# A two-layer hybrid backbone on one core: the same instructions, ordered by another scheduler model

## The chip, the cores and the metric

The kernel runs on one core of a Trainium2 chip. The metric is the device time of one execution in microseconds (us). Three timed runs of the kernel before took 2687.60, 2689.13 and 2694.43 us; the median, 2689.13, is the time that the prediction speaks of.

## What is computed

The input is 256 latent tokens and 256 context tokens of 1024 channels. Two layers of this block run one after the other, and a final RMSNorm gives the latent tokens:

```
h   = modulate(rmsnorm(x), shift, scale)              # adaLN: shift, scale, gate from c
u   = h @ w_in                                        # one combined input projection
mix = [rwkv7 (both directions), gla (both directions, chunks of 64),
       windowed attention (sink and context keys), s5 (both directions)]
y   = sum_i sigmoid(h @ w_gate_i) * (mix_i(u) @ w_branch_i)
x   = x + gate * (y @ w_out)
h2  = modulate(rmsnorm(x), ...)
x   = x + gate * moe(h2)    # top-1 group of 4, top-2 of its 8 experts, hidden 512
```

Everything is float32 to within its last bits: many products are done as a pair of a rounded part and its remainder (`hh`, `hl`; `yh`, `yl`; `bh`, `bl`).

## The kernel before, in words

`layer` (L1734) writes one layer down in this order: the first norm, the adaLN products (`adaln`, L1232: a 512 KB block of w_ada is loaded and meets eight small matmuls into `ada`, whose sum goes to `mods`), S5 (`s5`, L1033), GLA (`gla`, L634, with the chunk sums `pc<-cst,ke` at L731), the RWKV projections (`rwkv_in`), attention (`attn`), the eight RWKV units (`rwkv_units`, L360), and the gated merges of the four mixers (`merge`, L1336). Merges 1, 3 and 2 (GLA, S5, attention) need nothing of the units; merge 0 needs their output `yT[0]`. Then come the output projection and the second norm (`tail`, L1569) and the mixture of experts (`moe`, L1608; a pair of experts in `pair`, L1496). Layer 0 works on 512 tokens after the mixers, layer 1 on the 256 latent ones.

A unit (`rwkv_sub`, L463) is one half of the heads, one direction, one stream; there are 2 x 2 x 2 per layer, and here they are called U0 to U7 in layer 0 and V0 to V7 in layer 1. A unit is a long chain. TensorE makes scores (`psc`), VectorE and ScalarE copy them (`sm`), a DMA sends their diagonal blocks to device memory (`ad`, L510), another spreads them over the partitions (`lt`, L513), VectorE inverts the blocks in 62 operations of which each needs the one before:

```
for t in range(31):
    n = 31 - t
    self.tt(tm[:, :, 0:n], lt[...], ti[...], OP.mult)
    self.tt(ti[:, :, t + 1:32], ti[:, :, t + 1:32], tm[:, :, 0:n], OP.add)
```

DMAs bring the result back transposed (`td`, L524, and `tT`, L529), and TensorE runs eleven small groups (`psp`, `psy`, `psz`, `psv`, `psta`, `psav`, `pst`, `psq`, `psh`, `pss`, `psyo`) with copies by other engines between them. After every four units `rwkv_finish` (L410, matmuls `pc`) norms and gates a half. While a unit waits for VectorE or a DMA, TensorE has the merges' gate products to do: `pa`, sixteen or more matmuls for each 512 KB of gate weights (`g`, then the pair `gs`).

Nobody writes the order of the instructions by hand. The program is traced in the order of the code, and the tile layer's scheduler then picks, for each engine, the next instruction from those whose inputs and buffers its model of the machine has ready; where several are ready, the one that stands first in the code goes first. So the merges, which stand behind the units in the code, fill what the model thinks idle. Each engine, and each DMA queue (nearly all loads go through SP's), executes its list strictly in that order. The change touches the call that opens this scheduler, at L1869.

Of the kernel before, what the change touches and what calls it, by code (L numbers as in the profile page):

```python
# [46 lines left out]
def _consts():  # L47
# [3 lines left out]
    s = p % 64  # L51
# [15 lines left out]
    # sums of the four partial rows: row r of layer l  # L67
# [4 lines left out]
    # unit columns 4 (p % 8) .. + 3 of a 32-token block  # L72
# [14 lines left out]
def pack(i):  # L87
# [18 lines left out]
    def cols(a):  # L106
        """128 columns a tile: [l, n, 128, 8, 128]"""
        return a.reshape(L, 128, 8, -1, 128).transpose(0, 3, 1, 2, 4)

    def rows(a):  # L110
        """256 columns of half of the rows a tile: [l, n, 2, 128, 4, 256]"""
        return a.reshape(L, 128, 2, 4, -1, 256).transpose(0, 4, 2, 1, 3, 5)
# [6 lines left out]
    # query heads in the order 0, 2, 1, 3  # L119
# [53 lines left out]
class Net:  # L173
# [18 lines left out]
    def psum(self, name, **bufs):  # L192
        """A pool for the eight banks, cut into rotating sets."""
        self.pbufs = bufs
        cm = self.tc.tile_pool(name=name, bufs=1, space=PSUM, reuse_waits="tile")
        self.ps = cm.__enter__()
        return cm
# [4 lines left out]
    def const(self, c, n, pool):  # L202
        """Constants that one part alone needs."""
        t = pool.tile([128, n], F32, name="const")
        self.nc.scalar.dma_start(t, self.io["cst"][:, c:c + n])
        return t
# [10 lines left out]
    def wtile(self, src, pool):  # L217
        """A weight tile [128, k, n] of at most 8 KB on each partition."""
# [5 lines left out]
    def gload(self, src, pool=None):  # L224
        """A granule [128, k, n] of weights, of at most 4 KB on each partition."""
# [8 lines left out]
    def gsplit(self, src):  # L234
        """The granule as an exact pair for the tensor engine."""
# [10 lines left out]
    def mm3(self, out, a, b, start, stop):  # L246
        """Product of two exact pairs: all but the product of the two remainders, below float32's last bit."""
# [4 lines left out]
    def proj(self, out, src, h, a):  # L252
        """Channel-major projection: out = 128 columns of the weights, tokens a .. 511."""
# [7 lines left out]
    def rowpair(self, src):  # L261
        """256 columns of weights: the pair of each k."""
# [27 lines left out]
    # ------------------------------------------------------------------ RWKV  # L290
    def rwkv_in(self, l, h, lo, pool, tp, between):
        """Projection, centered shift and low-rank projections; what the units need."""
# [18 lines left out]
        # per-partition (scale, offset) that make the rate into the two stacked key factors  # L311
# [27 lines left out]
        # low-rank projections of xa  # L339
# [15 lines left out]
    def rwkv_first(self, l, st, pool):  # L355
        """What the first units need."""
# [23 lines left out]
    def unit_tiles(self, st, p0, pool, depth):  # L380
        """Tiles of the units whose constant parts are written once."""
# [16 lines left out]
    def rwkv_half(self, l, hf, st, pool):  # L398
        """Minus the normalized key direction of two heads."""
# [10 lines left out]
    def rwkv_finish(self, l, hf, st, y, pool):  # L410
        """Group norm over each head, gain, bonus, gate."""
# [23 lines left out]
    def rwkv_pre(self, hf, d, st, pool):  # L435
        """Decay and in-context rate of both streams, in scan order: the decays' products within a chunk,
        their inverses, and the two stacked key factors."""
# [19 lines left out]
        # the sums are used up: their place takes the first factor  # L457
# [5 lines left out]
    def rwkv_sub(self, hf, d, s, u, S0, st, na, y, pool):  # L463
        """One stream of one direction: four chunks of 64 tokens. S0: the state before it."""
# [28 lines left out]
        # scores (transposed) with token-major copies of the keys beside them  # L493
# [11 lines left out]
        # inverse of the 32-token diagonal blocks: four columns of one block a partition  # L505
# [24 lines left out]
        # off-diagonal quarter of the 64-token inverse  # L530
# [28 lines left out]
        # token-major values beside the solved block  # L559
# [13 lines left out]
        # banks of their own: their row tiles differ  # L573
# [31 lines left out]
        # states entering the chunks  # L605
# [27 lines left out]
    # ------------------------------------------------------------------ GLA  # L633
    def gla(self, l, h, yT, lo, pool):  # L634
# [8 lines left out]
        # low-rank decay input first: it heads the longest chain  # L643
# [29 lines left out]
        # log decays of both directions  # L673
# [29 lines left out]
    def gla_dir(self, d, la, q, kx, v, mg, oT, lo, pool):  # L703
# [23 lines left out]
        # per-chunk state increments  # L727
# [28 lines left out]
        # block-diagonal entering states of two heads; scores block-diagonal over the chunks of a token tile  # L756
# [41 lines left out]
    # ------------------------------------------------------------- attention  # L798
    def attn(self, l, h, yT, lo, pool):
# [8 lines left out]
        # queries and keys of a token tile, in places that the probabilities take later  # L808
# [34 lines left out]
        for a in range(2):  # L843
            ps = self.pa()
            for t in range(t0, 4):
                # heads a and a + 2: one for each key/value head
                nc.tensor.transpose(ps[:, 128 * t:128 * t + 128], qk[t][:, 128 * a:128 * a + 128], ident)
            self.act(qT[:, a, 128 * t0:512], ps[:, 128 * t0:512], AF.Copy, scale=0.125)
        # heads a + 2 g: a pair of row groups for the scores, of column groups for the sums
# [40 lines left out]
    # -------------------------------------------------------------------- S5  # L890
    def cmul(self, o, a, b, t, eng=None):
        """o = a * b for pairs (re, im) of views; t: two scratch views."""
# [8 lines left out]
    def sincos(self, out, ang, shift, pool, name):  # L901
        """out = sin(ang + shift), the angle reduced to [-pi, pi] in three exact steps."""
# [36 lines left out]
    def s5_params(self, l, ld, t2, pool):  # L939
        """Powers of the discrete transition, the input matrix and the chunk-scan tables."""  # L940
# [26 lines left out]
        # unit rotation over a chunk of eight tokens  # L967
# [5 lines left out]
        # (a - 1) / lam  # L973
# [25 lines left out]
    def s5_head(self, l, ld, pool):  # L999
        """What depends on the parameters alone."""  # L1000
# [12 lines left out]
    def s5_table(self, pr, d, pool):  # L1013
        """Powers 0 .. 63 of the rotation over a chunk."""
# [18 lines left out]
    def s5(self, l, h, w, yT, lo, pool, pr):  # L1033
# [6 lines left out]
        # chunks of eight tokens: ug[(t, channel), group, chunk]  # L1040
# [48 lines left out]
    def s5_quarter(self, d, gb, lo, pr, tb, ug, ys, kd, t2, dd, pool):  # L1089
        """One direction of eight groups: four pairs of groups."""  # L1090
# [20 lines left out]
        # input matrix times powers, in the order of a chunk's tokens  # L1111
# [9 lines left out]
        # impulse response within a chunk  # L1121
# [22 lines left out]
        # states at chunk ends, rotated into a frame where the scan is real  # L1144
# [13 lines left out]
        # z = f * conj(rotation)  # L1158
# [15 lines left out]
        # states entering each chunk, in token order  # L1174
# [21 lines left out]
        # within the chunk and from the entering state: banks of their own, their tiles differ  # L1196
# [22 lines left out]
    # --------------------------------------------------------- conditioning  # L1219
    def cond(self):  # L1220
        """silu of both conditioning vectors, channel-major, padded to a 32-column tile."""
# [10 lines left out]
    def adaln(self, l, js, pool=None, bank="A"):  # L1232
        """Tiles js of the layer's modulations. mods: rows (layer, modulation, stream), four partial sums of each."""
# [11 lines left out]
    def modcols(self, l, ks, mc, ps):  # L1245
        """Channel-major scale and shift of the first norm, mc: [128, scale/shift, stream, 8], for blocks ks."""
# [9 lines left out]
    def rstd(self, xs, pool, name, bufs=1):  # L1256
        """1 / rms of each token of the [128, 1024] tiles xs, by Newton's iteration."""
# [17 lines left out]
    def norm1(self, xs, xn, pool, then):  # L1275
        """Normalized tokens xn; then(k, their transposes in a PSUM bank)."""
# [13 lines left out]
    def modulate(self, k, mc, h, src, tmp):  # L1290
        """Modulated tokens as an exact pair."""
# [6 lines left out]
    def rows(self, l, pool):  # L1298
        """Rows of the modulations and of the second norm's scale, as exact pairs for the tensor engine."""
# [20 lines left out]
    def bcast(self, rw, r, half):  # L1320
        """PSUM bank holding half a row on every partition."""
# [6 lines left out]
    # ---------------------------------------------------------------- merge  # L1328
    def split(self, pool, tags, src, bufs=1, eng=None):
        """src as an exact pair for the tensor engine."""  # L1330
# [5 lines left out]
    def merge(self, l, i, h, yT, acc, lo, first, pool, between, pairs=None):  # L1336
        """acc (channel-major) += (1 + tanh(gate / 2)) * branch: twice the gated branch."""
# [27 lines left out]
    def project(self, t, w, acc, x, bs, lo, pool):  # L1365
        """x += modulation * (merged @ w_out) for a token tile."""
# [11 lines left out]
    # ------------------------------------------------------------------ MoE  # L1378
# [494 lines left out]
```

## Time and profile before

| | |
|---|---|
| median of three timed runs | 2689.13 us |
| span of the profiled execution | 2682.7 us |
| outside the span, against the median | 6.4 us |
| TensorE (PE) busy | 2425.7 us, 90% |
| VectorE (DVE) busy | 1257.7 us, 47% |
| ScalarE, GpSimd busy | 651.6 and 708.5 us |
| moved by DMA | 553.6 MB, 206 GB/s on the mean |

The profiled execution has no time of its own beside its span; all sums are made against the span. From the timeline, in us from the span's start: layer 0 has its front (norm, adaLN, S5, GLA, RWKV projections, attention) to 364, the units with the merges to 646, the last merge to 785, the tail to 882 and its experts to 1480; layer 1 has its front to 1785, the units to 2079, the last merge to 2116, the tail to 2180 and the experts to the end. TensorE is the engine that is nearly always busy, so the time is its work plus its idle stretches; each of these has a reason that a view of the waits names.

### The profile page before, as it was taken

To read this page: it belongs to the slowest core of one execution; us is meant where nothing else is said; L and a number is where in the kernel's file an instruction comes from. 1 tells how busy PE (TensorE), PEld (TensorE's weight loads), DVE (VectorE), ACT (ScalarE), POOL (GpSimd) and SP (SyncE) were. 2 spreads that over 40 slices of the span, in tenths; PEclk is the share of its full clock that TensorE was granted. 3 is DMA by queue.
4 is the path that set the end of the run, shared out by engine and by line. 5 is a ranking of instruction groups with operands and counts; after the bars stand their busy time and mean duration, and the time that the engine had idled before them with its cause. 6 is when DMAs were issued, how large, how long until landed. Compare 5 with 4: busy or idle time off the path is not lost. (4 is left out here: it accounts for less than half of the span.)

```text
span 2682.7 us, 41783 instructions
## 1 busy us (share of the span) xinstructions
PE 2425.7 (90%) x16663; PEld 1460.5 (54%) x16663; DVE 1257.7 (47%) x3477; ACT 651.6 (24%) x1147; POOL 708.5 (26%) x609
## 2 busy tenths in 40 slices
PE   6889989989898999999998788987988989999997
PEld 5766756567654545444443676765766644333332
DVE  6575488883224433222223766478665342212212
ACT  2232543222212111111111332441222311111111
POOL 2224411133421233133313333431133411111121
PEclk8987989999999899999999887887688989999999
DMA  6332212124543698888884342322222779999994
GB/s 218 105 112 87 67 49 66 51 63 161 200 149 115 278 390 345 312 333 325 325 347 196 114 143 84 115 64 72 62 81 64 255 310 419 411 395 402 399 398 172
DMA packets 143947, 553.59 MB, mean 206 GB/s; under 512 B 33236, under 2 KB 64340, under 8 KB 93316
## 3 DMA queue, kind: packets, MB, share of 16 engines
q1 hardware_dynamic: 138480, 544.88, 53.9%
q10 hardware_dynamic: 5268, 5.97, 0.7%
q8 instruction: 135, 2.21, 0.3%
q14 instruction: 64, 0.52, 0.1%
HBM read 546.66 MB, written 4.13 MB: 205 GB/s over the span
## 5 line engine op out<-in xcount | busy, mean ns | idle before, releaser
L267 PE MATMUL pa<-hh,gs 128*128 128x512 f32 (+2 forms) x1440 | 446.6, 383 | 19.5 <-DVE sg L283 8.6
L273 POOL TENSOR_TENSOR gs<-g,gs 128x1024 fp32r<-128x1024 f32 (+1 forms) x106 | 255.4, 2413 | 570.5 <-PE pa L267 271.2
L273 POOL TENSOR_TENSOR ta<-ta,mb 128x512 f32<-128x512 f32 x93 | 127.8, 1381 | 834.4 <-ACT ta L270 834.4
L267 PEld LDWEIGHTS pa<-hh,gs 128*128 128x128 f32 (+1 forms) x1440 | 270.6, 202 | 83.2 <-issue 15.8
L267 PE MATMUL pd<-w,hT 128*64 128x512 f32 x1024 | 276.6, 599 | 13.1 <-ACT hT L270 12.4
L267 PE MATMUL pa<-hl,gs 128*128 128x512 f32 (+2 forms) x720 | 270.9, 387 | 0.0
L267 PE MATMUL pgate<-w,xT 128*64 128x512 f32 x1024 | 251.3, 596 | 0.0
L267 PE MATMUL pup<-w,xT 128*64 128x512 f32 x1024 | 249.2, 594 | 0.0
L267 PEld LDWEIGHTS <-h2p 128*128 128x128 bf16 x2304 | 134.3, 99 | 77.9 <-issue 72.5
L270 ACT ACTIVATE gs<-g 128x1024 fp32r<-128x1024 f32 (+1 forms) x106 | 110.4, 1045 | 258.0 <-PE pa L267 175.9
L267 PE MATMUL pg<-oh,h2p 128*128 128x128 bf16 x2304 | 162.6, 222 | 5.8 <-DVE nv L1652 4.2
L267 PEld LDWEIGHTS pa<-hl,gs 128*128 128x128 f32 (+1 forms) x720 | 148.1, 206 | 28.3 <-issue 9.6
L267 PEld LDWEIGHTS pd<-w,hT 128*64 128x64 f32 x1024 | 81.6, 136 | 146.7 <-issue 124.3
L267 PEld LDWEIGHTS pup<-w,xT 128*64 128x64 f32 x1024 | 78.4, 137 | 143.1 <-issue 138.9
L267 PEld LDWEIGHTS pgate<-w,xT 128*64 128x64 f32 x1024 | 74.8, 137 | 139.6 <-issue 129.4
L267 PE MATMUL py<-yp,oT 128*128 128x512 f32 x384 | 132.2, 438 | 11.2 <-ACT ta L270 5.1
L283 DVE SCALAR_TENSOR_TENSOR hd<-hd,pgate 128x512 f32<-128x512 f32 x32 | 22.0, 687 | 246.4 <-ACT hd L270 246.3
L273 DVE TENSOR_TENSOR tm<-lt,ti 128x76 f32<-128x76 f32 (+27 forms) x496 | 132.3, 286 | 5.9 <-DMA lt<-ad 0.8
L273 DVE TENSOR_TENSOR ti<-ti,tm 128x76 f32<-128x76 f32 (+28 forms) x496 | 128.1, 277 | 5.0
L273 DVE TENSOR_TENSOR hd<-hd,pup 128x512 f32<-128x512 f32 x32 | 22.0, 687 | 218.0 <-PE pup L267 218.0
L273 POOL TENSOR_TENSOR x<-x,ta 128x512 f32<-128x512 f32 x93 | 121.5, 1313 | 4.9
L283 DVE SCALAR_TENSOR_TENSOR yp<-pd,ws,yp 128x512 fp32r<-128x512 f32 x64 | 47.7, 746 | 152.6 <-ACT yp L270 152.6
(495 smaller groups left out, 3736.2 us busy)
## 6 DMA issues: line engine op xcount, KB each, us to landing
w<-in_w_g SPq DMA_DIRECT2D x128, 1024.0 KB, 8.2
w<-in_w_d SPq DMA_DIRECT2D x128, 1024.0 KB, 10.2
w<-in_w_u SPq DMA_DIRECT2D x128, 1024.0 KB, 8.5
g<-in_w_ada SPq DMA_DIRECT2D x96, 512.0 KB, 3.8
g<-in_w_in_gate SPq DMA_DIRECT2D x64, 512.0 KB, 3.6
g<-in_w_in_rwkv SPq DMA_DIRECT2D x16, 512.0 KB, 3.6
lt<-ad SPq DMA_DIRECT2D x16, 512.0 KB, 4.4
wb<-in_w_branch SPq DMA_DIRECT2D x64, 128.0 KB, 3.0
```

The source lines that it names most:

```text
L267: self.nc.tensor.matmul(out, lhsT, rhs, start=start, stop=stop, skip_group_check=True)
L270: self.nc.scalar.activation(out, in_, f, **kw)
L273: (eng or self.nc.vector).tensor_tensor(out, a, b, op)
L283: self.nc.vector.scalar_tensor_tensor(out, a, s, b, op0=op0, op1=op1)
```

## The change

The scheduler that orders the instructions is told to use its event-by-event model of all devices (engines, queues and semaphores) in place of its plain model. That is one argument. The rest of the diff takes out comments and docstrings and leaves blank lines in their place, so that line numbers stay.

```diff
-    with tile.TileContext(nc) as tc:
+    with tile.TileContext(nc, schedule_with_timeline_sim=True) as tc:
         build(tc, nc, io, out)
```

Both programs hold the same 20,889 instructions, with the same names, on the same engines; what differs is each engine's order (and, with it, the number of waits that stand apart as instructions: 494 and 461 on PE, 364 and 351 on DVE, 731 and 759 on SP). Three places on PE show what moves.

The first is the end of the units of layer 1, on PE. `tT_15196` belongs to V6 and `tT_15197` to V7; `ar_15192` and `ar_15193` likewise; `pa` is merge work. Before:

```order
L267 MATMUL pa<-hh,gs 128x256
L267 MATMUL psq<-sm,x_15194 64x64
L267 MATMUL psp<-cst,tT_15197 32x32 x7
L267 MATMUL pa<-hl,gs 128x256
L267 MATMUL pa<-hh,gs 128x256 x2
L267 MATMUL psq<-sm,x_15194 64x64 x7
L267 MATMUL psh<-x_15194,sm 64x64 x8
L267 MATMUL psy<-tp,sm 32x32 x8
L267 MATMUL pa<-hh,gs 128x256 x4
L267 MATMUL pss<-h_16884,qg 64x64 x2
```

And now:

```order
L267 MATMUL psc<-ar_15192,bk 128x192 x2
L267 MATMUL psc<-ar_15193,bk 128x192 x8
L267 MATMUL psp<-cst,tT_15196 32x32 x8
L267 MATMUL psy<-tp,sm 32x32 x8
L267 MATMUL psz<-tT_15196,ysb 32x32 x8
L267 MATMUL psv<-cst,vv 64x64 x8
L267 MATMUL psta<-cst,ar_15192 64x64 x8
L267 MATMUL psav<-x_15194,sm 64x64 x8
L267 MATMUL psp<-cst,tT_15197 32x32
L267 MATMUL pst<-bk,tT_15196 64x128 x8
L267 MATMUL psp<-cst,tT_15197 32x32 x7
```

The scores of V7 are now directly ahead of V6's `psp`, and no merge matmul stands between there and V7's finish; before, 161 `pa` matmuls stood between V7's scores and its `psp` and 245 up to its finish. The merge work that stood here has been moved ahead of V7's scores.

The second is the end of the units of layer 0, on PE (`tT_3388` belongs to U6, `x_3386` to U6, `x_3387` and `tT_3389` to U7). Before:

```order
L267 MATMUL pa<-hh,gs 128x512 x5
L267 MATMUL pst<-bk,tT_3389 64x128 x8
L267 MATMUL pa<-hh,gs 128x512 x2
L267 MATMUL pa<-yh,bh 128x512
L267 MATMUL pa<-yl,bh 128x512
L267 MATMUL psq<-sm,x_3387 64x128
L267 MATMUL pa<-yh,bl 128x512
L267 MATMUL pa<-yh,bh 128x512
L267 MATMUL psq<-sm,x_3387 64x128 x7
```

And now:

```order
L267 MATMUL pa<-hh,gs 128x512 x8
L267 MATMUL psp<-cst,tT_3388 32x32 x8
L267 MATMUL psy<-tp,sm 32x32 x8
L267 MATMUL psz<-tT_3388,ysb 32x32 x8
L267 MATMUL psv<-cst,vv 64x64 x8
L267 MATMUL psta<-cst,ar_3383 64x64 x8
L267 MATMUL psav<-x_3386,sm 64x64 x8
L267 MATMUL pst<-bk,tT_3388 64x128 x8
L267 MATMUL psq<-sm,x_3386 64x128 x8
L267 MATMUL psh<-x_3386,sm 64x64 x8
```

From U7's last scores there are 35 merge matmuls up to the first row of this piece, and none from it to U7's finish; then 14 are left of merges 1 to 3. Before, 174 merge matmuls stood between U7's scores and its finish, and 238 of merges 1 to 3 behind it.

The third is the end of merge 0 in layer 0, on PE: adaLN products of layer 1's modulation that are spread through merge 0. `pa<-w,acc` is the output projection of the tail; eight `ada` matmuls use one 512 KB block. Before:

```order
L267 MATMUL pb<-yl,bh 128x512
L267 MATMUL pb<-yh,bl 128x512
L267 MATMUL bs<-mods,cst 128x512 x2
L267 MATMUL ada<-g,cT 32x128 x8
L267 MATMUL pa<-w,acc 128x512
L267 MATMUL bs<-mods,cst 128x512 x2
L267 MATMUL mod<-mods,cst 12x512
L267 MATMUL pa<-w,acc 128x512
```

And now:

```order
L267 MATMUL pb<-yl,bh 128x512
L267 MATMUL pb<-yh,bl 128x512
L267 MATMUL pa<-w,acc 128x512 x4
L267 MATMUL ada<-g,cT 32x128 x16
L267 MATMUL pa<-w,acc 128x512 x12
L267 MATMUL ada<-g,cT 32x128 x32
L267 MATMUL bs<-mods,cst 128x512 x2
L267 MATMUL ada<-g,cT 32x128 x32
L267 MATMUL bs<-mods,cst 128x512 x2
L267 MATMUL mod<-mods,cst 12x512
```

Ten blocks of w_ada are now used behind merge 0's last matmul, and one was before.

## Rows read from the trace of the kernel before

**Rows 1.** The page, busy time of an engine, share of the span, instructions.
```profile
PE 2425.7 (90%) x16663; PEld 1460.5 (54%) x16663; DVE 1257.7 (47%) x3477; ACT 651.6 (24%) x1147; POOL 708.5 (26%) x609
```

**Rows 2.** Busy time by stretch: units with merges, of layer 0 and layer 1.
```profile
core 0: us, PE busy (x) PEld busy (x) DVE busy (x) ACT busy (x) POOL busy (x), PEclk, DMA share, GB/s
364.00:785.00 421.00, 389.84 (x2984) 272.93 (x2981) 247.96 (x792) 112.29 (x196) 123.67 (x67) 0.95 0.36 117
...
1785.00:2116.00 331.00, 285.57 (x2441) 227.94 (x2440) 216.76 (x738) 88.95 (x166) 103.14 (x69) 0.80 0.32 97
```

**Rows 3.** Timeline around U7, layer 0: start, length, engine, line, operation.
```profile
562.82 0.92 PE L267 MATMUL psc<-ar,bk 64*128 64x192 f32 x4
...
568.09 0.56 SPq L513 DMA_DIRECT2D lt<-ad  x1
...
601.62 0.17 DVE L273 TENSOR_TENSOR ti<-ti,tm 128x4 f32<-128x4 f32 x1
...
609.49 0.43 PE L267 MATMUL psp<-cst,tT 32*32 32x32 f32 x14
...
644.06 0.39 PE L267 MATMUL pa<-hl,gs 128*128 128x512 f32 x1
644.29 0.39 PE L267 MATMUL pa<-hh,gs 128*128 128x512 f32 x1
...
644.84 1.12 PE L267 MATMUL pc<-sg,g 64*128 64x512 f32 x2
```

**Rows 4.** The page: groups of the 62 operations, and the DMA of lt.
```profile
L273 DVE TENSOR_TENSOR tm<-lt,ti 128x76 f32<-128x76 f32 (+27 forms) x496 | 132.3, 286 | 5.9 <-DMA lt<-ad 0.8
L273 DVE TENSOR_TENSOR ti<-ti,tm 128x76 f32<-128x76 f32 (+28 forms) x496 | 128.1, 277 | 5.0
...
lt<-ad SPq DMA_DIRECT2D x16, 512.0 KB, 4.4
```

**Rows 5.** Busy time by stretch: U7's and V7's chain, and V7's last part.
```profile
564.00:646.00 82.00, 73.30 (x631) 51.31 (x631) 55.31 (x172) 21.75 (x35) 24.14 (x13) 0.96 0.20 60
...
2000.00:2078.50 78.50, 64.44 (x620) 53.65 (x621) 49.99 (x165) 20.16 (x33) 26.36 (x19) 0.85 0.30 87
2049.00:2078.50 29.50, 29.50 (x341) 22.87 (x338) 10.81 (x28) 10.29 (x16) 7.75 (x6) 1.00 0.16 46
```

**Rows 6.** PE groups by line: units' second parts (15 groups), a finish (3 groups).
```profile
L267 PE MATMUL psq<-sm,x 128*64 128x128 f32 (+1 forms) x256 | 23.6, 279 | 2.0 <-DVE x L589 2.0
...
L267 PE MATMUL pc<-s,cst 128*128 128x512 f32 (+1 forms) x16 | 7.6, 559 | 4.8 <-DVE s L283 4.8
...
L267 PE MATMUL pc<-yT,cst 128*128 128x512 f32 (+1 forms) x8 | 3.7, 548 | 0.0
...
L267 PE MATMUL psyo<-qg,h 64*64 64x64 f32 x16 | 1.5, 267 | 0.0
```

**Rows 7.** Timeline: PE's weight loads at a switch between a unit and a merge.
```profile
562.82 0.62 PEld L267 LDWEIGHTS psc<-ar,bk 64*128 64x128 f32 x4 [0.17 <-ACT sm L270]
...
563.66 0.19 PEld L267 LDWEIGHTS pa<-hh,gs 128*128 128x128 f32 x1 [0.22 <-issue]
```

**Rows 8.** Timeline at the end of merge 0, layer 0: adaLN products and their loads.
```profile
744.57 0.64 PE L267 MATMUL ada<-g,cT 128*32 128x128 f32 x16
746.50 0.64 PE L267 MATMUL ada<-g,cT 128*32 128x128 f32 x16
...
751.80 28.48 SPq L231 DMA_DIRECT2D g<-in_w_ada  x10
```

**Rows 9.** Waits of PE: layer 1's front, then layer 0's experts (us, times, longest).
```profile
PE pc L731 <- POOL ke L273: 8.9, 1, 8.9
...
PE ph L1538 <- DVE hd L273: 7.8, 10, 0.8
...
PE pd L267 <- ACT hT L270: 4.9, 10, 0.7
```

**Rows 10.** Busy time by stretch, layer 1's units; the clock is third from the end.
```profile
1785.00:1990.00 205.00, 176.96 (x1501) 134.30 (x1499) 150.65 (x548) 52.19 (x101) 47.53 (x32) 0.74 0.25 70
...
1840.00:1860.00 20.00, 17.62 (x232) 14.07 (x230) 16.08 (x57) 4.93 (x9) 5.45 (x3) 1.00 0.35 100
1860.00:1900.00 40.00, 36.09 (x286) 27.51 (x288) 24.41 (x103) 5.60 (x14) 5.33 (x4) 0.55 0.13 36
```

## The prediction, made before the changed kernel ran

> **What bounds the kernel now.** First the page's busy times: TensorE is at 2425.7 us [rows 1] of a span of 2682.7, so 257 us of idle TensorE are all that an order can win, unless it alters how long the matmuls take. No instruction is added or dropped, so every term below is idle time that comes or goes, and the clock. Second, busy time by stretch: the units with their merges take 421.0 us in layer 0 with TensorE busy 389.8 (31.2 idle), and 331.0 us in layer 1 with 285.6 (45.4 idle) [rows 2]. These are the stretches in which the scheduler has most freedom. Third, the timeline of one unit. U7's last scores end at 563.7, its `lt` load is issued at 568.1, its last inversion step ends at 601.8, `psp` is at 609.5 and its finish ends at 646.0 [rows 3]. That is 82 us of chain, beside which TensorE was busy for 73.3 us. V7's chain takes 78.5 us, with 64.4 us of TensorE work beside it [rows 5]. So a unit's chain is long and almost free of charge, as long as merge work lies beside it. The question to put to the new order is how much of that work still lies there.
>
> **The length of the chain when nothing lies beside it.** From last scores to the first inversion step: issue of `lt` 4.4 us after the scores end [rows 3], landing 4.4 [rows 4], 8.8 together. The 62 steps: 31 x (286 + 277) ns = 17.4 us [rows 4]. From the last step to `psp`'s end: 601.8 to 609.9, 8 us [rows 3]. From there to the finish: 29.5 in layer 1 [rows 5]. Sum 63.7 us, the lower end. The upper end is what was measured with work beside it and another unit's steps taking turns on VectorE: 82 and 78.5 us.
>
> **What now lies beside it.** In layer 0 the order leaves 35 merge matmuls behind U7's scores, which follow each other at 0.23 us (644.06 and 644.29) [rows 3]: 8.1 us. Then U6's and U7's second parts: 15 groups of rows, from 23.6 to 1.5 us for 16 units, sum 180.5, so 11.3 us a unit [rows 6], and a finish, three groups of 7.6, 4.2 and 3.7 us for four finishes, 3.9 us [rows 6]. Together 8.1 + 22.6 + 3.9 = 34.6 us. The chain of 64 to 82 us leaves TensorE idle for 29 to 47. I take 40: U6's scores end over 20 us of matmuls ahead of U7's, so its steps are half done when U7's begin. In layer 1 there is no merge matmul at all: 22.6 + 3.9 = 26.5 us, and idle for 37 to 52. I take 50, near the upper end, since the scores of V6 end only one scores group (3 us) ahead of V7's, so that both units' 35 us of steps share VectorE just as in the measured 78.5 us. What waits behind is everything: PE's list is in order, and merge 0 needs the finish anyway.
>
> **What the moved merge work gives back.** It now lies ahead, among the earlier units, where it covers waits. Of the 31.2 idle us of layer 0's stretch 8.7 lie beside U7's chain (82.0 less 73.3), so 22.5 elsewhere; of layer 1's 45.4, 14.1 beside V7's (78.5 less 64.4), so 31.3 elsewhere [rows 2, 5]. I let 9 and 12 of these remain; the ends are none and all. Then layer 0's stretch goes from 31 to 49 (+18) and layer 1's from 45 to 62 (+17).
>
> **Fewer changes of work.** The new order has TensorE go from merge to unit matmuls or back 116 times in place of 198 in layer 0, and 114 in place of 188 in layer 1. A switch left the weight load idle for 0.17 and 0.22 us [rows 7], of which a part is a true wait; I take half, 0.11: -9 and -8 us. The ends are 0 and -34 for both.
>
> **The adaLN blocks behind merge 0.** Ten blocks of w_ada are used behind merge 0's last matmul in place of one, with only 16 projection matmuls among them. In the trace ten such loads took SP 28.5 us to issue, each waiting for one of two buffers, and the closest blocks ran 1.9 us apart (744.57 and 746.50) [rows 8]. Ten blocks need 19 to 28 us; beside them lie ten times 0.64 us of `ada` and 16 x 0.23 of projection, 10 us. So 9 to 18 us of idle, or none, if loads run ahead or if the second norm has TensorE wait there anyway. I take 12. Before, the same loads were hidden by merge 0's matmuls; that cover is what goes.
>
> **Layer 1's front.** The one long stall there is 8.9 us, `pc` for GLA's `ke` [rows 9], which VectorE reached late because S5's steps stood ahead. The new order moves GLA's steps ahead of more of S5's and puts the first `pc` seven rows earlier, with S5 and adaLN matmuls in place of a bare run of `pa`. -9 us, the ends 0 and -9 (the wait can only go once). Layer 0's front changes as much but had short waits; I take nothing.
>
> **The experts.** The gather of the next pair now stands between `pup` and `ph` or `ph` and `pd` for three more pairs in each layer. The waits it can cover are 7.8 and 4.9 us over ten pairs in layer 0 [rows 9]: three pairs, -4 us. Layer 1's experts are paced by their weight loads; nothing.
>
> **The sum.** +18 +17 -9 -8 +12 -9 -4 = +17 us on a profiled execution of 2682.7, so 2699.7; with the 6.4 us between span and median, 2706 us.
>
> **The clock.** In layer 1's units the granted clock was 0.74 of full on the mean, and it alternated between stretches at the upper of its two levels (1840 to 1860: 1.00, TensorE busy 17.6 of 20) and stretches near the lower one (1860 to 1900: 0.55, busy 36.1 of 40, when it was hardly idle) [rows 10]. So in this trace a dense stretch was not always a fast one, and I put the clock at no change. The bounds: at 0.95, as in layer 0's same stretch [rows 2], the 177 us of matmuls would be 177 x (1 - 0.74/0.95) = 39 us shorter at most; at half clock for the whole of layer 1's merge 0 behind its gap, which takes 36 us now, up to 36 longer. The Trainium skill ("Perfetto Trace Analysis", Matmul Optimizations) says that the engine scales with utilization and that matmuls should run back to back in batches; by that rule the longer batches of the new order would raise the clock, and the first rival below is what comes of it. The skill's "TensorE: Matmul & The Clock Gate" (Part 1, HAM oscillation) speaks the other way: work that follows a wait starts cold, which would make the two long gaps dearer than their own length. The row of 1860 to 1900 agrees with neither by itself.
>
> **The rivals.**
> (a) Faster. The denser filler ahead of V7 lifts layer 1's clock to layer 0's 0.95. Its place is 1785 to 1990, its price -39, and it decides as soon as it gives over 25 us. Sum +17 - 39 = -22: 2667 us. For it: the waits of that stretch are ones that filler covers. Against: the 0.55 at 90% busy.
> (b) No change. U7's and V7's gaps come out at the lower ends (29 and 37, not 40 and 50), and the adaLN blocks hide in the norm's wait: 17 - 11 - 13 - 12 = -19, against which the other waits of the units stay at half (+6) and the switches give nothing back (+17): +4, 2693 us.
> (c) Much slower. Upper ends for the gaps (47 and 52), no stall covered elsewhere (22.5 and 31.3), 18 us for the adaLN blocks: (69.5 - 31.2) + (83.3 - 45.4) + 18 - 17 - 13 = +64, 2753 us. Against: merge matmuls really are put ahead of the earlier units' waits.
> (d) The order is hardly different where it counts, so the change does nothing: excluded by the rows of the order, where hardly a row of PE stands as it did.
>
> **How the numbers follow.** A measurement of this kernel can tell about 0.3% (8 us) from no change: 2681 to 2697. Forecast (2698 to 2732) 0.40; (a) and what lies between it and no change 0.29; (b) and other sums within the 8 us 0.20; (c) 0.11. Faster 0.29, same 0.20, slower 0.51. The range leaves a tenth at either end: half of (a) lies above 2662, and (c) reaches past 2745.
>
> **What would show it.** Right: in the changed trace a gap of 25 us or more on TensorE in each layer with nothing but `ti` and `tm` on VectorE, and `psp` of U6 and V6 released by `tT`; `ada` waiting for `g<-in_w_ada` for about 10 us ahead of layer 0's tail; `psc` waiting less in sum than before; the 8.9 us for `ke` gone. Wrong: TensorE's idle time in 364 to 785 and 1785 to 2116 no larger than 31 and 45 us, or TensorE's busy time changed by over 15 us, which would be the clock.

## The result

The changed kernel takes 2704.1 us (median of 20 runs), the kernel before 2687.5 (median of 20 beside it). The ratio is 1.0067, 95% interval 1.0049 to 1.0084: slower by 0.7%, where 2706 was forecast. How it comes about is another matter, and most of this part is about that. The profiled execution has a span of 2708.3, 25.6 more than the one of before, where the medians differ by 17; the stretches below are compared between these two executions. One kernel's runs differ too (the 20 of the kernel before lie between 2669 and 2698 us), so a few us in a stretch can be chance. The page:

```profile
PE 2419.9 (89%) x16663; PEld 1463.3 (54%) x16663; DVE 1273.8 (47%) x3477; ACT 649.3 (24%) x1147; POOL 692.3 (26%) x609
```

Over the whole run TensorE is busy for 5.8 us less than before [rows 1], so in sum the loss is idle time; by stretch it is not. The ends are those of the same instructions in both traces (by them layer 0's experts end at 1472.6 us before and layer 1's tail at 2170.0, where the overview of the kernel before gave 1480 and 2180). Times are in us; TensorE's idle and busy time are read from the rows under the table, those of before first. The forecast was one of idle time.

| stretch | before | after | difference | idle | busy | forecast |
|---|---|---|---|---|---|---|
| layer 0, start to the tail's end | 881.3 | 928.4 | +47 | +21 | +26 | +18 -9 +12 = +21 |
| layer 0, experts | 591.3 | 588.7 | -3 | -6 | +3 | -4 |
| layer 1, front | 312.1 | 284.2 | -28 | -11 | -17 | -9 |
| layer 1, units to V7's finish | 293.7 | 294.8 | +1 | +18 | -17 | +17 -8 = +9 |
| layer 1, merge 0 and tail | 91.6 | 109.4 | +18 | +13 | +5 | 0 |
| layer 1, experts | 498.6 | 487.5 | -11 | -4 | -7 | 0 |
| sum | 2668.6 | 2693.0 | +24 | +31 | -6 | +17 |

```profile
core 0: us, PE busy (x) PEld busy (x) DVE busy (x) ACT busy (x) POOL busy (x), PEclk, DMA share, GB/s
0.00:881.30 881.30, 787.59 (x5817) 553.74 (x5818) 516.14 (x1560) 262.51 (x468) 246.26 (x221) 0.92 0.34 112
881.30:1472.60 591.30, 568.05 (x3528) 256.15 (x3524) 174.67 (x296) 97.63 (x161) 161.15 (x122) 0.99 0.80 320
1472.60:1784.70 312.10, 265.87 (x2188) 206.77 (x2187) 202.59 (x561) 109.74 (x200) 107.16 (x130) 0.83 0.32 102
1784.70:2078.40 293.70, 251.60 (x2187) 195.93 (x2187) 202.94 (x718) 75.54 (x141) 77.14 (x52) 0.78 0.26 74
2078.40:2170.00 91.60, 78.13 (x394) 55.95 (x394) 38.15 (x99) 25.95 (x44) 34.46 (x24) 0.90 0.72 267
2170.00:2668.60 498.60, 474.47 (x2565) 191.95 (x2562) 117.37 (x230) 77.97 (x129) 79.75 (x61) 1.00 0.91 373
```
```profile
0.00:928.40 928.40, 814.04 (x5804) 577.93 (x5804) 535.84 (x1558) 261.69 (x467) 240.63 (x221) 0.87 0.32 106
928.40:1517.10 588.70, 571.19 (x3534) 252.94 (x3534) 164.11 (x299) 97.92 (x161) 156.16 (x123) 0.99 0.83 322
1517.10:1801.30 284.20, 249.32 (x2203) 194.21 (x2202) 207.56 (x561) 110.83 (x202) 103.51 (x130) 0.87 0.34 111
1801.30:2096.10 294.80, 234.53 (x2219) 186.07 (x2215) 215.74 (x718) 73.89 (x142) 79.26 (x54) 0.81 0.26 74
2096.10:2205.50 109.40, 82.88 (x345) 58.54 (x344) 36.07 (x97) 25.34 (x42) 32.83 (x22) 0.77 0.58 224
2205.50:2693.00 487.50, 467.52 (x2564) 193.64 (x2565) 107.67 (x231) 77.07 (x129) 76.76 (x60) 0.99 0.93 382
```

So the sum came out right, and the idle time came out within 9 us of the forecast wherever the forecast named a term. What it left out is the idle time in layer 1's merge 0 and tail, and the busy time: nearly the same matmuls took longer in layer 0 and less long in layer 1. The experiments below repeat the split. Layer 1's units are idle for 41 to 43 us and busy for 244 to 253 in the three traces where they have the order of before; in the ten where they have the new order unmended, they are idle for 58 to 68 and busy for 228 to 235. Busy time by stretch of the changed kernel, the answer to [rows 2, 5, 10]: the units up to U7's last scores, U7's chain, merge 0 and the tail of layer 0; the units up to V7's last scores and V7's chain of layer 1.

```profile
378.60:657.90 279.30, 264.65 (x1926) 193.22 (x1922) 200.03 (x562) 84.47 (x149) 82.42 (x45) 0.95 0.23 69
657.90:727.80 69.90, 47.85 (x415) 33.00 (x415) 36.47 (x127) 9.94 (x18) 6.44 (x4) 0.58 0.12 35
727.80:840.40 112.60, 93.33 (x660) 65.37 (x660) 21.59 (x41) 17.09 (x25) 31.08 (x18) 0.91 0.65 235
840.40:928.40 88.00, 83.29 (x248) 43.81 (x240) 41.51 (x122) 22.26 (x33) 13.55 (x8) 0.81 0.29 110
1801.30:2036.10 234.80, 204.98 (x1863) 164.40 (x1859) 185.09 (x575) 66.02 (x127) 78.41 (x52) 0.87 0.31 89
2036.10:2096.40 60.30, 29.85 (x356) 21.67 (x356) 30.65 (x143) 7.87 (x15) 1.15 (x2) 0.58 0.06 14
```

The two forecast gaps are there: TensorE is idle for 22 us beside U7's chain and for 30 beside V7's. But the granted clock, third from the end, tells as much: it is 0.58 beside both chains, where it was 0.96 and 0.85 before [rows 5], and 0.87 in layer 1's units ahead of V7's, where it was 0.75. Of the units ahead of the two chains in the kernel before:

```profile
364.50:564.00 199.50, 185.20 (x1493) 123.79 (x1493) 160.90 (x563) 60.48 (x115) 39.73 (x21) 0.92 0.22 62
1784.70:2000.00 215.30, 187.26 (x1568) 142.39 (x1567) 152.97 (x554) 55.38 (x108) 50.79 (x34) 0.75 0.25 70
```

The timeline of V7's gap:

```profile
2034.42 1.64 PE L267 MATMUL psc<-ar,bk 64*128 64x192 f32 x4 [3.07 <-ACT sm L270]
2056.14 0.31 PE L267 MATMUL psp<-cst,tT 32*32 32x32 f32 x2 [20.08 <-DMA tT<-td]
```

TensorE has nothing between V7's scores and V6's `psp`, as the order said. Beside U7's chain there is no such single wait: the longest is 6.1 us, and the 22 us are many small ones, not the unbroken gap of 25 us that the prediction named as a sign. Waits that are larger or smaller than before (whole run; the kernel before, then the changed one):

```profile
PE ada L267 <- DMA g<-in_w_ada: 35.7, 14, 17.1
PE pa L267 <- POOL gs L273: 11.7, 11, 2.3
PE psp L267 <- DMA tT<-td: 8.1, 5, 4.7
```
```profile
PE psp L267 <- DMA tT<-td: 35.9, 10, 20.1
PE ada L267 <- DVE cT L273: 24.5, 1, 24.5
PE pa L267 <- ACT gs L270: 21.6, 7, 6.3
PE ada L267 <- DMA g<-in_w_ada: 20.8, 15, 6.6
...
PE pc L731 <- POOL ke L273: 2.6, 2, 1.7
```

The 8.9 us for `ke` in layer 1 [rows 9] are down to 0.9 (the longer of the two waits left is one in layer 0). The wait for `tT` is four times as long, that for `gs` (gate weights made ready too late) about twice. At the start TensorE waited 17.1 us for the first block of w_ada and now waits 24.5 for `cT`.

### The profile page after: what moved, and what is told of

Read it like the earlier page. It is cut to its first block, busy times and chain, and to the rows that moved or that the text cites. A ratio compares the mean times of both kernels' runs of the same rounds, so it can differ in the third digit from the quotient of the medians.

```text
span 2708.3 us, 41764 instructions
## 1 busy us (share of the span) xinstructions
PE 2419.9 (89%) x16663; PEld 1463.3 (54%) x16663; DVE 1273.8 (47%) x3477; ACT 649.3 (24%) x1147; POOL 692.3 (26%) x609
## 5 line engine op out<-in xcount | busy, mean ns | idle before, releaser
L267 PE MATMUL pa<-hh,gs 128*128 128x512 f32 (+2 forms) x1440 | 434.5, 379 | 26.6 <-ACT gs L270 21.6
L273 POOL TENSOR_TENSOR ta<-ta,mb 128x512 f32<-128x512 f32 x93 | 120.9, 1310 | 834.6 <-ACT ta L270 834.5
L267 PE MATMUL pgate<-w,xT 128*64 128x512 f32 x1024 | 276.3, 600 | 0.0
L267 PE MATMUL pd<-w,hT 128*64 128x512 f32 x1024 | 260.2, 598 | 4.3 <-ACT hT L270 4.3
L267 PE MATMUL pa<-hl,gs 128*128 128x512 f32 (+2 forms) x720 | 261.5, 375 | 0.0
L267 PE MATMUL pup<-w,xT 128*64 128x512 f32 x1024 | 260.2, 595 | 0.0
L283 DVE SCALAR_TENSOR_TENSOR yp<-pd,ws,yp 128x512 fp32r<-128x512 f32 x64 | 47.9, 749 | 242.2 <-ACT yp L270 242.2
L273 DVE TENSOR_TENSOR tm<-lt,ti 128x124 f32<-128x124 f32 (+27 forms) x496 | 131.0, 278 | 30.5 <-DMA lt<-ad 23.0
L273 DVE TENSOR_TENSOR ti<-ti,tm 128x124 f32<-128x124 f32 (+27 forms) x496 | 139.9, 297 | 8.4
```

The costliest lines, as they stand in the source:

```text
L267: self.nc.tensor.matmul(out, lhsT, rhs, start=start, stop=stop, skip_group_check=True)
L273: (eng or self.nc.vector).tensor_tensor(out, a, b, op)
L283: self.nc.vector.scalar_tensor_tensor(out, a, s, b, op0=op0, op1=op1)
```

## The experiments

In most of them parts of one order are put into the other. Each engine's list is held by edges without waits: they fix what the scheduler issues first and add nothing that the chip waits for. `pin` holds a set of instructions to the relative order that they had before, engine by engine; `hold` puts some instructions of an engine behind one of its own. Each ratio is against the kernel before on the same chip; the changed kernel's is 1.0067.

```diff
+def pin(tc, nc, text):     # text: the instructions of each engine, in the order of before
+    ...
+            tc.add_manual_dep(i, last, DependencyInfo(NoSync, DATA), reason="pin")
+            last = i.name
+def hold(tc, nc, first, then):
+    for k in then:
+        tc.add_manual_dep(by[k], first, DependencyInfo(NoSync, DATA), reason="hold")
```

### e1: layer 0 as before

```diff
+        if l == 0: pin(tc, nc, <all of layer 0>)
```

> The event-by-event model orders the program, but layer 0 is held, engine by engine, to the order that it had before (edges without waits); layer 1 keeps the event model's order. By the prediction's steps layer 1's part of the change is +17 (units) -8 (switches) -9 (GLA) = 0: about 2687 us, the same as before, and the whole cost sits in layer 0. By the two traces layer 1 took 1196 us before and 1176 after, 20 less: if that is the order's doing, and not one run's chance, this kernel takes about 2668 us, ratio 0.993.

2683.0 us, ratio 0.9974 (0.9949 to 0.9999). Layer 1's new order is worth a small gain, if any, between the two expectations, and the changed kernel's whole loss sits in layer 0.

### e2: layer 1 as before

```diff
+        if l == 1: pin(tc, nc, <all of layer 1>)
```

> The opposite half: layer 0 in the event model's order, layer 1 held to the order of before. By the prediction's steps layer 0's part is +18 -9 +12 -4 = +17: 2704 us, ratio 1.006. By the two traces layer 0 took 44 us longer: about 2731 us, ratio 1.016. If the two halves add up, this and the kernel with layer 0 held differ from before by amounts whose sum is the +17 of the whole change.

2728.9 us, ratio 1.0134 (1.0081 to 1.0187): about 36 us slower than before, near the larger expectation. The two halves, -7 and +36, add up to +29; with their intervals this agrees with the change's +18. Layer 0's forecast of +17 was too small by half.

### e3: the gap of layer 0 mended

```diff
+        if l == 0: hold(tc, nc, <U7's last psc>, <the last 230 pa of merges 1 to 3>)
```

> The changed kernel with one thing put back: the last 230 merge matmuls of layer 0 are held behind U7's last scores (edges without waits), so that 126 merge matmuls lie between U7's scores and its psp and 90 more before its finish (35 and 0 in the changed kernel, 110 and 64 before). Theory: the empty stretch at the end of the units costs what it leaves TensorE idle or slow, 25 to 40 us of which the earlier units take some back: the kernel gets 15 to 30 us faster than the changed one, to about 2680 us. Rival: the idle time only moves, since the merge work held back is then missing beside U0 to U5, whose waits grow: no change, 2704 us within 5.

2712.0 us, ratio 1.0078 (1.0050 to 1.0105): nothing gained. The gap is filled and U7's scores come 30 us earlier (620 in place of 650 in e2's trace, where layer 0 has the changed order), but U7's finish stays at 720 us, as in e2's. By stretch:

```profile
372.90:500.00 127.10, 118.11 (x883) 87.00 (x881) 99.07 (x279) 43.28 (x77) 33.32 (x18) 0.96 0.24 67
500.00:620.00 120.00, 104.46 (x859) 74.92 (x858) 82.46 (x250) 29.90 (x56) 27.95 (x16) 0.86 0.21 61
620.00:719.60 99.60, 86.31 (x598) 60.00 (x597) 52.04 (x159) 20.62 (x34) 26.35 (x15) 0.84 0.21 59
```

The work that was held back is now missing at 500 to 620, where TensorE is idle for 15.5 us at a clock of 0.86; in e2's trace it is idle there for 5.6, at 0.95. The rival was right.

### e4: the gap of layer 0 made in the kernel before

```diff
-    with tile.TileContext(nc, schedule_with_timeline_sim=True) as tc:
+    with tile.TileContext(nc) as tc:
+        if l == 0: hold(tc, nc, <pa 160, 100, 51 from the end>, <U6's psc, U7's psc, U7's last psc>)
```

> The kernel before, with its plain model, and only U6's and U7's scores held behind the merge matmuls that stand ahead of them in the changed order: 36 merge matmuls are left between U7's scores and its psp, none up to its finish, as in the changed kernel (36 here, 35 there). The rest of layer 0 and all of layer 1 stay in the order of before. Theory: this alone gives layer 0's main term, 15 to 30 us slower than before (about 2710 us). Rival: the cost of layer 0 comes from the general mixing of the units and merges or from its front, and this gives under 8 us.

2723.9 us, ratio 1.0140 (1.0095 to 1.0185): 38 us slower, more than the upper expectation. Such a gap alone (31 us idle in the second row):

```profile
500.00:650.00 150.00, 142.28 (x900) 102.50 (x897) 73.97 (x181) 41.91 (x69) 56.15 (x30) 0.95 0.23 68
650.00:742.00 92.00, 60.64 (x465) 40.67 (x463) 42.05 (x141) 12.43 (x22) 10.10 (x6) 0.65 0.13 37
```

So a gap can be dear. Here the merge work that left it went where no wait needs it (a solid block at 571 to 622, between U5 and U6); in the changed kernel it goes among U0 to U5. That this is why the gap is dear here is argued and not shown.

### e5: layer 0 from the units on as before

```diff
+        if l == 0: pin(tc, nc, <units, merges, tail, experts of layer 0>)
```

> Layer 0's front (norm, adaLN, S5, GLA, projections, attention) stays in the event model's order; its units, merges, tail and experts are held, engine by engine, to the order of before; layer 1 stays in the event model's order. Holding only the merge matmuls behind U7 (e3) gave nothing, so the question is whether the loss of layer 0 lies in its units as a whole or ahead of them. Theory: the order of units and merges as a whole (gap, small waits and the lower clock that follows them) costs 30 us, the front about 10: this kernel takes 2692 us, 12 less than the changed one and about 10 more than the one with all of layer 0 held. Rival: the front is what delays everything, and this kernel stays at 2704.

2668.7 us, ratio 0.9923 (0.9894 to 0.9952): faster than the kernel before, and by 14 us faster than with all of layer 0 held. So the units, merges and tail of layer 0 cost the changed kernel 39 us (1.0067 less 0.9923). By these times the new front of layer 0 would be a gain; the traces do not bear that out. Layer 0's tail ends at 873 us in this one, but at 881 to 892 in those of e10 to e12 (below), which hold layer 0 in the same way, and at 881 to 890 in the four where all of layer 0 has the order of before (before, e1, e7, e8). The same work in five traces, from the end of S5 and GLA to the end of the tail, first the kernel before, then this one, the changed one, the made gap (e4), and merge 0 as before (e9, below):

```profile
276.40:881.30 604.90, 559.42 (x3763) 379.65 (x3764) 339.98 (x1051) 178.70 (x336) 167.68 (x104) 0.95 0.32 104
```
```profile
285.00:872.50 587.50, 544.06 (x3674) 367.82 (x3672) 334.80 (x1047) 169.87 (x323) 154.26 (x98) 0.94 0.32 104
```
```profile
292.00:928.40 636.40, 571.81 (x3673) 390.37 (x3672) 356.90 (x1049) 170.60 (x323) 151.59 (x98) 0.87 0.28 95
```
```profile
276.20:921.30 645.10, 576.88 (x3764) 390.74 (x3761) 343.36 (x1050) 179.24 (x336) 167.21 (x104) 0.90 0.30 98
```
```profile
293.20:911.70 618.50, 551.83 (x3674) 379.48 (x3672) 352.45 (x1047) 170.72 (x323) 151.58 (x98) 0.90 0.30 99
```

Take the second and the third, which do the same 3674 matmuls: 49 us apart, 21 of them idle time (43.4 and 64.6) and 28 busy time. No matmul was added, so these 28 are the same matmuls taking longer, at a mean clock of 0.87 and not 0.94. The event model's front does 89 matmuls more ahead of this stretch, in 8 us.

### e6: the start mended

```diff
+        if l == 0: hold(tc, nc, <cth on ScalarE>, <what before had behind it>)
```

> The changed kernel with one thing put back at its start: on ScalarE the tanh of the conditioning vector (cth), which all adaLN products wait for, is issued ahead of the loads and activations that the event model put before it, as in the order of before (edges without waits). In the changed trace cT is ready at 24.4 us and the first adaLN product starts at 24.1 instead of 17.1. Theory: TensorE starts 7 to 9 us earlier and the time falls by as much, to about 2696 us. Rival: the loads of w_ada or the norm hold the front anyway, and nothing is gained (2704).

2716.6 us, ratio 1.0084 (1.0052 to 1.0115): nothing gained. TensorE starts at 14.1 us in place of 24.5, held until then by the first block of w_ada, and waits 11.4 us more for later blocks (25.5 in all):

```profile
PE ada L267 <- DMA g<-in_w_ada: 25.5, 7, 14.1
```

The rival was right: with `cT` early, it is the loads that hold the front's start.

### e7: the gap of layer 1 mended

```diff
+        if l == 0: pin(tc, nc, <all of layer 0>)
+        if l == 1: hold(tc, nc, <V7's last psc>, <the last 320 pa of merges 1 to 3>)
```

> Layer 0 held to the order of before, layer 1 in the event model's order but with the last 320 merge matmuls held behind V7's last scores, so that 204 lie between the scores and psp and 110 more before the finish (0 and 0 without it, 167 and 78 before). The kernel to compare with is the one with layer 0 held, 2683 us. Theory: the 36 us in which TensorE is idle beside V7's chain, and the slow clock there, are refilled: 10 to 25 us faster than that one, about 2665. Rival, as in layer 0: the work held back is missing earlier, and nothing is gained (2683, within 5).

2683.6 us, ratio 0.9980 (0.9954 to 1.0006), the same as with layer 0 held alone (0.9974). Layer 1 from its units' start to the tail's end, first with the gap (e1), then with the gap mended (e7):

```profile
1769.10:1989.00 219.90, 193.48 (x1841) 156.88 (x1841) 185.31 (x559) 65.71 (x124) 77.87 (x51) 0.92 0.32 93
1989.00:2064.40 75.40, 39.01 (x372) 27.66 (x372) 35.69 (x159) 8.81 (x19) 1.22 (x2) 0.54 0.08 19
2064.40:2173.00 108.60, 80.94 (x349) 56.51 (x349) 36.46 (x99) 25.31 (x42) 32.53 (x22) 0.78 0.59 225
```
```profile
1768.40:1966.00 197.60, 163.96 (x1507) 127.67 (x1505) 160.76 (x548) 51.06 (x102) 49.32 (x31) 0.75 0.26 73
1966.00:2063.00 97.00, 78.78 (x708) 65.97 (x708) 53.28 (x170) 24.11 (x41) 30.34 (x22) 0.89 0.26 77
2063.00:2170.40 107.40, 81.35 (x347) 56.23 (x347) 36.18 (x98) 25.35 (x42) 32.84 (x22) 0.79 0.60 228
```

The filling empties the first stretch: its clock falls from 0.92 to 0.75, and its idle time goes from 26 to 34 us although it does 334 matmuls less. From the units' start to V7's finish (the first two rows of each) TensorE is idle for 11 us less than with the gap and busy for 10 us more, and the finish comes 1 us earlier. So V7's gap is paid back by what its filler does ahead of it, and nearly all of that pay is busy time at the faster clock.

### e8: the early loads of layer 1 held back

```diff
+        if l == 0: pin(tc, nc, <all of layer 0>)
+        if l == 1: hold(tc, nc, <merge 0's last gate load on SP>, <six loads of w_g, w_u>)
```

> Layer 0 held to the order of before, layer 1 in the event model's order but with the six 1 MB expert loads that stand ahead of merge 0's last gate and branch loads on SP's queue held behind them. The kernel to compare with is the one with layer 0 held, 2683 us. In the changed trace merge 0 of layer 1 takes 55 us against 37, TensorE waiting for gs, and the experts 488 us against 499. Theory: both come from these six loads: merge 0 gets 10 to 15 us shorter, the experts, which are paced by their loads, about 10 longer; in sum 2680 within 6. Rival: the experts' gain has another cause and stays: 2670.

2673.7 us, ratio 0.9934 (0.9909 to 0.9959), 11 us less than e1. Merge 0:

```profile
2070.50:2112.30 41.80, 31.50 (x207) 29.79 (x207) 15.51 (x17) 11.85 (x23) 25.14 (x15) 0.73 0.73 274
```

It takes 41.8 us in place of 54.4 in e1, and the experts stay at 488 us. So the loads cost merge 0 13 us and give the experts nothing; the theory was right on the first and wrong on the second.

### e9: merge 0 and the tail of layer 0 as before

```diff
+        if l == 0: pin(tc, nc, <merge 0 and tail of layer 0>)
```

> The changed kernel, with only merge 0 and the tail of layer 0 held among themselves to the order of before (the adaLN blocks spread through merge 0 again, the loads of both in their old order); the units, with the gap at U7's end, stay as the event model has them. In the trace with layer 1 held plain, merge 0 and the tail took 200.7 us from U7's finish, and 179.3 us for the same work before. Theory: this order (ten adaLN blocks behind the merge, gate pairs gs that come late) is the largest part of layer 0's loss: 15 to 22 us faster than the changed kernel, about 2686. Rival: the 21 us are the gap's aftermath (a lower clock, loads that the gap held up) and stay: 2704.

2715.0 us, ratio 1.0124 (1.0075 to 1.0172): by the time, nothing gained. By the trace the stretch is 18 us shorter than in the changed kernel (618.5 and 636.4 above; 193.0 in place of 200.9 from U7's finish on). But layer 1's front, whose matmuls stand within 4 of 2204 places of those in the changed kernel on the mean, takes 304 us in this trace and 284 in the changed one, which takes it back. What makes that front so touchy stays open; the test of the adaLN term alone is inconclusive by its time.

### e10: the parts that paid, together

```diff
+        if l == 0: pin(tc, nc, <units, merges, tail, experts of layer 0>)
+        if l == 1: pin(tc, nc, <merge 0 and tail of layer 1>)
```

> The parts that paid, together: layer 0's units, merges, tail and experts and layer 1's merge 0 and tail held to the order of before; layer 0's front, layer 1's front, units and experts in the event model's order. e5 (2669 us) holds all of this but layer 1's merge 0 and tail, which take 109 us in the event order and 92 before. Theory: 12 to 17 us less than e5, about 2655, ratio 0.987. Rival: the loads that are then issued later are missed by the experts, which give back the gain: 2668.

2652.9 us, ratio 0.9888 (0.9846 to 0.9930): the fastest of all, 33 us under the kernel before on the same chip and 51 under the changed kernel's median. Merge 0 and the tail of layer 1 take 89.9 us in its trace, 91.6 before, 109.4 in the changed kernel, and the experts give back 2 us (489.5, 487.3 in e5's trace).

### e11: layer 1's experts as before

```diff
+        if l == 0: pin(tc, nc, <units, merges, tail, experts of layer 0>)
+        if l == 1: pin(tc, nc, <experts of layer 1>)
```

> e5 with layer 1's experts also held to the order of before. These experts took 499 us in every trace with the plain order and 488 in every trace with the event order, and the six early loads were not the reason (e8). Theory: the order inside the experts (the gathers of the next pair ahead of ph and pd) is: the kernel gets about 10 us slower than e5, 2679. Rival: the gain comes from what runs ahead of the experts, and this stays at e5's 2669.

2683.3 us, ratio 0.9988 (0.9961 to 1.0015), 15 us more than e5. The experts, first here, then in e5:

```profile
2175.70:2674.50 498.80, 474.50 (x2565) 192.17 (x2565) 117.31 (x231) 77.97 (x129) 79.51 (x61) 0.99 0.91 373
```
```profile
2161.30:2648.60 487.30, 467.19 (x2564) 193.21 (x2565) 107.72 (x233) 76.88 (x129) 76.81 (x60) 0.99 0.93 382
```

11.5 us from the order inside the experts alone, as the theory said; the same loads then move at 382 in place of 373 GB/s.

### e12: layer 1's front as before

```diff
+        if l == 0: pin(tc, nc, <units, merges, tail, experts of layer 0>)
+        if l == 1: pin(tc, nc, <front of layer 1>)
```

> e5 with layer 1's front (adaLN, S5, GLA, projections, attention) also held to the order of before. That front took 312 us before and 293 in e5's trace: 10 us less idle (the 8.9 us wait for ke among it) and 9 us less busy. Theory: the order of the front is worth 15 to 20 us: 2686. If only the ke wait is the order's doing, 9 us: 2678.

2702.7 us, ratio 1.0054 (1.0026 to 1.0083): 34 us more than e5, far more than `ke`'s 9. The front takes 328.6 us here, 292.9 in e5's trace:

```profile
1478.30:1806.90 328.60, 273.97 (x2219) 215.63 (x2218) 213.25 (x608) 111.44 (x206) 107.56 (x131) 0.81 0.32 100
```
```profile
1463.90:1756.80 292.90, 256.52 (x2199) 199.14 (x2201) 213.80 (x562) 111.12 (x203) 105.01 (x132) 0.84 0.34 109
```

36 us, of which 18 are idle time and 17 busy time at a lower clock. Not all of e12's 34 us is that order: layer 0, held alike in both, ends 14 us later in this trace than in e5's. And part of the 36 is not the front's order itself: 20 matmuls and 46 VectorE operations of the units, which stay free, now lie in the stretch. Where the whole of layer 1 had the order of before, the front took 312 to 314 us (three traces); in the event order it took 281 to 304 (ten traces). So the order is worth some 20 us there and not 36.

## Why the prediction came out right

**The size and the sign were right, in part by luck.** The forecast is a sum of idle time. Where it named a term, the idle time came near it: +21 for +21 in layer 0 up to its experts, -6 for -4 in these, -11 for -9 in layer 1's front, +18 for +9 in its units. Two things were left out: 13 us of idle time in layer 1's merge 0 and tail, and the busy time, which rose by 26 us in layer 0 up to its experts and fell by 17, 17 and 7 in parts of layer 1. That the busy time comes to -6 in sum is no doing of any step. The experiments bear the places out: the new order of layer 0's units, merges and tail costs 39 us (e5 against the changed kernel), layer 1's merge 0 and tail cost 9 to 18 (e10, e8 and the table), layer 1's front gains some 20 (e12 and the traces) and its experts 11 (e11). No run measures the two terms for fewer changes of work (-9 and -8) by themselves.

**The gaps.** The mechanism was right: a chain with too little work beside it. U7's chain took 70 us and V7's 60, the latter under the lower end of 64. But the idle time beside them was 22 and 30 us, not 40 and 50. Beside U7's the work that was summed to 34.6 us took 47.9 at a clock of 0.58; beside V7's the chain itself was shorter than the 76 us to which 26.5 and 50 add up. The other step that failed is "I let 9 and 12 of these remain", the give-back. Ahead of the two chains TensorE is idle for 15 and 30 us in the changed kernel and was for 14 and 28 before, though much more merge work lies there now: none of it was given back as idle time. Gaps that came out too small and a give-back that did not come made up for each other in the sum. In layer 1 the moved work gave back busy time instead, at the faster clock; e7, which puts it back, gains 11 us of idle time and loses 10 of busy time. That layer 0's loss is its units, merges and tail is shown; that it is the gap is not: filling the gap gains nothing (e3), and e4 shows only that such a gap can cost 38 us.

**The adaLN blocks.** +12 was forecast. `ada` waits for its loads for 8.7 us behind U7's finish, just under the 9 to 18; and new is a wait of 10.1 for `gs`, which I had not looked for: when merge 0 starts, its gate weights are not there. Merge 0 and tail together took 200.9 us, 21 more than the 179.3 of about the same work before; e9 gives 8 of it back.

**The clock was the term that I set to zero.** Of the 49 us between the changed kernel and e5 in layer 0, 28 are busy time. I had bounded the clock from both sides (39 less, 36 more) and put it at no change because the bounds were alike. Both sides came true, the gain in layer 1's units and the loss in layer 0 and beside the two chains. The sign that I had named for it, busy time changed by over 15 us, shows in three of the six stretches and not in the sum. Behind U7's chain, the matmuls of merge 0 first follow each other at 0.43 us and from 737 us on at 0.23, the lower and the upper of the clock's two levels:

```profile
735.29 0.63 PE L267 MATMUL pa<-hh,gs 128*128 128x512 f32 x1
735.72 0.63 PE L267 MATMUL pa<-hl,gs 128*128 128x512 f32 x1
...
737.08 0.39 PE L267 MATMUL pa<-hl,gs 128*128 128x512 f32 x1
737.30 0.40 PE L267 MATMUL pa<-hh,gs 128*128 128x512 f32 x1
```

The two rules of the Trainium skill that I set against each other each describe one side. "TensorE: Matmul & The Clock Gate" (Part 1, HAM oscillation), work behind a wait starts cold, agrees with these rows: merge 0 starts at the lower level behind a chain full of waits. "Perfetto Trace Analysis" (Matmul Optimizations), matmuls back to back in batches, agrees with e1 against e7 (0.92 with the filler, 0.75 without), and not with the 0.55 at 90% busy in the kernel before [rows 10].

**Layer 1's front and experts.** For the front I counted one wait of 8.9 us; 8 of it went, and the idle time fell by 11 in all. The other 17 us are busy time, at a clock of 0.87 in place of 0.83. For the experts, "paced by their weight loads; nothing" is the step that failed: the order inside them is worth 11 us (e11). Why is open. `pd` waits for `hT` 0.7 us in place of 7.6 before, but `pw` now waits 6.1 for `oT`; 7 of the 11 us are busy time at a like clock; and whether the loads, at 382 in place of 373 GB/s, are cause or consequence no run tells.

**Rivals.** (a), the faster clock in layer 1's units, happened in part (0.87 ahead of V7's chain, of the 0.95 that it named; 17 us of its 39) and was spent on the idle time. (b) had smaller gaps, and (c) no stall covered elsewhere; both of these came true, and the sums of (b) and (c) missed because they did so together.

## What to carry to other kernels

A scheduler's model can serve one stretch better and another worse, and one argument mixes both: measured by stretch, the better order of most gave 1.1% less than the kernel before, where the change as a whole gave 0.7% more. An empty place in an order is not a price by itself; ask what the work that left it covers now, since in e3 and e7 filling it again emptied another place. And cost the busy time as well as the idle time: here it moved by up to 26 us in a stretch, and a forecast that adds up only idle time was right because these movements happened to cancel.

## What was not expected of the hardware

The granted clock moved whole stretches: the same 3674 matmuls of layer 0 took 544 and 572 us of busy time, at 0.94 and 0.87 of the upper level, and layer 1's units 252 and 235, at 0.78 and 0.81. Layer 1's front took anything from 281 to 304 us in the ten traces with an order of the event model. Three of these (e5, e10, e11) have one and the same order there on TensorE and took 293, 285 and 288. The experts of layer 1 took 498.6 to 498.8 us in four traces with one order and 487.3 to 489.5 in ten with the other.
